# Attention values projected by token for all heads at once, in place of one head pair at a time with transposes

## The chip, the cores and the metric

The kernel runs on one core of a Trainium2 chip. The metric is the device time of one execution in microseconds (us); a median of several runs is given where there is one. Instructions are named by the engine that runs them: PE (TensorE, the matmuls), DVE (VectorE), ACT (ScalarE), POOL (GpSimd) and SP (SyncE, which here issues all the transfers).

## The reference, cut to what matters

One decoder block over 512 tokens of width 1024. The part that the change touches is the start: a norm, one wide projection, and attention over 8 heads of width 64.

```python
h = rms_norm(x, attn_norm_g[i])
u = h @ w_in[i]
u_sb, u_rw, u_gate = jnp.split(u, [SB_COLS, SB_COLS + RW_COLS], axis=-1)
q, k, v = jnp.split(u_sb.reshape(bsz, seq, 3 * SB_HEADS, SB_HEAD_DIM), 3, axis=2)
o_sb = stick_breaking_attention(q, k, v).reshape(bsz, seq, SB_WIDTH)
o_rw = rwkv7_time_mix(u_rw, ...)
```

In the attention, the weights of a block of queries are multiplied with the values: `einsum('bhqk,bhkd->bhqd', w, v)`. Behind it come a recurrent branch (`rwkv7_time_mix`), gates, an MLP and gated embeddings, and a last norm. All inputs and the output are float32.

## The kernel before

**Number format.** Every large product is made of three matmuls, because an operand is held as a high part (`hi`, fp32r) and a rest (`lo`): `hi*hi`, `hi*lo` and `lo*hi`. One such triple over 128 rows of the contraction and 512 columns is called a *step* below. `mm3` (L186 to L194) makes a step with the weights as the stationary operand, so its output has features on the partitions and tokens along the row; `rows3` (L201 to L209) makes two steps with 128 tokens of `h` as the stationary operand and the weights streaming, so its output has tokens on the partitions. A unit of weights is 128 x 1024 numbers: it comes by one transfer (`load_to`, L162), is split by one ACT copy (L175) and one DVE subtraction (L176), and serves 8 steps.

**The norm.** `h_hi` and `h_lo` hold x times the gain, without the norm's factor. The factor `rs`, one number per token, is worked out while the first products run (`rstd_of`, L260) and multiplied in when a product leaves PSUM. It lies as a [128, 512] tile with the same row of 512 tokens on each partition.

**Attention, stage 1.** The heads go in four pairs `hp`. A pair needs three units: queries, keys, values. `projected` (L390 to L416) takes a finished product out of PSUM: for queries and keys it multiplies by `rs` and splits into `hi` and `lo`; for values it only makes `vT` (L414), features by tokens. Three steps later `token_major` (L417 to L426) turns `vT` with four PE transposes (L421) and splits the result into `vv` (ACT L424, DVE L425), tokens by features. `scores` (L445) and `attend` (L484) then run for each of the 8 heads; `attend` multiplies the weights with `vv` (L497) and adds the two halves of its output into `oo` (ACT L518, DVE L519), and behind every second head a transfer writes `oo` to memory (L521).

**What sets the order.** Before the loop over the heads, the queries and keys of pair 0 (16 steps) and the values of pair 0 (8 steps) are written out. All further projections (`early`, L548) come from one generator: pairs 1 to 3 (72 steps) and then the first five units of the recurrent branch (40 steps, `early_mixes`), 112 steps in all. `drive` (L284) shares the text out between the attention of a head and 11 steps of this generator (`NSTEP = 11`), nine times: once beside the first scores, and once per head. The 13 steps that are left follow behind the last head (L573). The order on each engine is near this order of the text, but not the same: an instruction whose operands come late is set behind others that are ready. Weights are fetched two units ahead, in the order of the list `seq`.

**PSUM and SBUF.** PSUM has 8 banks: two for projections (`ps_m`), five for scores (`ps_z`), one for the output of the attention (`ps_o`). The buffers of stage 1 (`p1`) are given back as a whole when the stage ends; the buffers of stage 2 (`p2`) lie where they were.

**Stage 2, the recurrent branch.** It begins with two small products per pair (L619, L620), for which `lora_w` and `t12` are split (ACT L608, L611; DVE L609, L613). For each pair, `prepare` and `scan` make a long chain of small instructions; beside them `fill` runs the remaining projections, listed in `FILL`, five or more units for each of the five rounds, and last the product of the attention's output (`U_UPSB`). The chain ends with `o_rw` (L993), whose split (`orw`, L221 and L222) feeds the first product of stage 3.

Of the kernel before, what the change touches and what calls it, by code (L numbers as in the profile page):

```python
# [18 lines left out]
P = 128  # L19
# [66 lines left out]
def tile_block(ctx: ExitStack, tc: tile.TileContext, xT, xt, pT, wts, lora, cols_d, gfin_d, consts_d, out, dbg=None):  # L86
# [41 lines left out]
    for hp in range(HP):  # L128
        seq += [(U_QKV, hp), (U_QKV, 4 + hp), (U_QKV, 8 + hp)]
# [71 lines left out]
    def rows3(ps, w, rhs, tt, k, first, last, cs=slice(0, 512)):  # L201

        xh, xl = (r[:, :, tt * P:(tt + 1) * P] for r in rhs)
        for j in range(2):
            wh, wl = (p_.rearrange("p (j f) -> p j f", j=2)[:, j, cs] for p_ in w)
            pe.matmul(ps, xh[:, k + j], wh, start=first and j == 0, stop=False, skip_group_check=True)  # L206
# [70 lines left out]
    with ExitStack() as sA:  # L277
# [43 lines left out]
        with ExitStack() as s1:  # L321
# [62 lines left out]
            heads, late = {}, []  # L384
# [5 lines left out]
            def projected(hp, i, ps):  # L390

                if i == 0:
                    t = p1.tile([P, T], F32, name="qT", tag="qkv", bufs=3)
# [10 lines left out]
                elif i == 1:  # L404
                    t = p1.tile([P, T], F32, name="kT", tag="qkv", bufs=3)
# [6 lines left out]
                else:  # L412
                    t = p1.tile([P, T], F32, name="vT", tag="qkv", bufs=3)
                    dve.tensor_tensor(out=t, in0=ps, in1=rs, op=ALU.mult)  # L414
                    late.append([3, hp, t])

            def token_major(hp, t):  # L417

                ps = psm.tile([P, T], F32, name="ps_m")
                for j in range(4):  # L420
                    pe.transpose(out=ps[:, j * P:(j + 1) * P], in_=t[:, j * P:(j + 1) * P], identity=ident)  # L421
                vv = p1.tile([P, 4, 2, 2, 64], F32R, name="vv")
                ps4 = ps.rearrange("p (j h d) -> p j h d", j=4, h=2)
                act.copy(out=vv[:, :, :, 0, :], in_=ps4)  # L424
                dve.tensor_tensor(out=vv[:, :, :, 1, :], in0=ps4, in1=r32(vv[:, :, :, 0, :]), op=ALU.subtract)  # L425
                heads[hp] += [vv, p1.tile([P, T], F32, name="oo", bufs=1)]  # L426

            def projections(hp, which=range(3)):
                for i in which:
                    w = weights(U_QKV, i * 4 + hp)  # L430

                    ps = psm.tile([P, T], F32, name="ps_m") if (hp, i) > (1, 0) else ps_z()
# [51 lines left out]
            def attend(hp, hh, got):  # L484

                vv, oo = heads[hp][3:]
# [6 lines left out]
                def output(js):  # L493

                    for j in js:
                        for part in (wh, wl):
                            pe.matmul(ps_o[:, j * P:T], vv[:, j, hh, :, :].rearrange("p a d -> p (a d)"),  # L497
# [29 lines left out]
            pss = [psm.tile([P, T], F32, name="ps_m") for _ in range(2)]  # L527
# [3 lines left out]
            v = projections(0, (2,))  # L531
# [21 lines left out]
            def with_late(steps):  # L553

                for _ in steps:
                    for l in late[:]:
                        l[0] -= 1
                        if l[0] < 0:
                            late.remove(l)
                            token_major(*l[1:])  # L560
                    yield

            heads_ = [(hp, hh) for hp in range(HP) for hh in range(2)]
            parts = {g: {} for g in heads_}
            ahead = with_late(early())
            NSTEP = 11
            drive((3, scores(*heads_[0], parts[heads_[0]])), (NSTEP, islice(ahead, NSTEP)))
            for n, g in enumerate(heads_):
                todo = [(5, attend(*g, parts[g])), (NSTEP, islice(ahead, NSTEP))]
# [796 lines left out]
def layout(i):  # L1366
# [14 lines left out]
    def rows(w):  # L1381
# [7 lines left out]
        U_QKV: units(w_in[:, 0:1536]),  # L1389
# [36 lines left out]
```

## Time and profile before

| | us |
|---|---|
| median of 3 runs | 870.2 |
| lowest and highest | 869.28, 870.54 |
| profiled execution, its own time | 869.75 |
| its span from the first to the last instruction | 867.7 |
| PE busy in the span | 851.4 (98%) |
| DVE busy | 678.1 (78%) |
| ACT busy | 448.6 (52%) |
| POOL busy | 80.4 (9%) |

The profile is of one execution. A row of instructions gives the line of the kernel, the engine, the operation, the output, the inputs and the shape; then the count, the busy time and the mean duration. A row of the timeline gives start, duration, engine, line, operation, output and inputs, and in brackets how long the engine had been idle before and who released it. Matmuls overlap in their pipeline, so what a matmul costs is the distance from its start to the next start, not its duration.

### The profile page before, as it was taken

What the parts mean: (1) busy time and instruction counts of PE and PEld (TensorE: products, weight loads), DVE (VectorE), ACT (ScalarE), POOL (GpSimd) and SP (SyncE); (2) the same over time, 40 slices, a digit from 0 to 9 for tenths busy, and PEclk for the clock granted to TensorE, in tenths of its full rate; (3) what the DMA queues carried; (4) which work ended last, traced back from release to release, by engine and by line L of the source; (5) the groups of instructions that cost most, each with busy time, mean ns of one, the idle gap of its engine ahead of it and who ended that gap; (6) DMA issues with size and microseconds to landing.
All of it is one profiled execution on the core that took longest, in us unless ns stands there. A gap on an engine that the chain in (4) does not pass through costs nothing.

```text
span 867.7 us, 13424 instructions
## 1 busy us (share of the span) xinstructions
PE 851.4 (98%) x5182; PEld 686.8 (79%) x5182; DVE 678.1 (78%) x1228; ACT 448.6 (52%) x703; POOL 80.4 (9%) x138
## 2 busy tenths in 40 slices
PE   8999999999999999999999999999999999999996
PEld 5778787877777777777888888888888888888885
DVE  7899987896979888776754789858985987697767
ACT  6888887744335343534424464344434543453744
POOL 1432431002302111020000000000000000000000
PEclk9999999999999999999999999999999999999999
DMA  7212212221121224437935621531252034300422
GB/s 269 98 49 66 82 62 85 74 97 51 62 87 57 80 73 153 141 116 258 318 121 181 232 73 38 182 120 49 83 184 98 25 127 164 98 1 0 170 73 98
DMA packets 32272, 95.32 MB, mean 110 GB/s; under 512 B 3664, under 2 KB 3664, under 8 KB 32208
## 3 DMA queue, kind: packets, MB, share of 16 engines
q1 hardware_dynamic: 32208, 94.46, 32.6%
q8 instruction: 41, 0.67, 0.3%
q14 instruction: 23, 0.19, 0.1%
HBM read 83.96 MB, written 10.49 MB: 109 GB/s over the span
## 4 chain that ended last, share of the span: by engine, by line
PE 81%; DVE 10%; ACT 4%; issue 1%; DMA 1%; SPq 0%; POOL 0%; POOLq 0%; DVEq 0%; ACTq 0%
PE ps_m L191 13%; PE ps_m L193 13%; PE ps_m L192 13%; PE ps_m L206 9%; PE ps_m L207 9%; PE ps_m L208 9%; DVE w_lo L176 2%; PE ps_g L817 1%; PE ps_o L497 1%; PE ps_g L193 1%; PE ps_c L935 1%; PE ps_s L944 1%; PE ps_g L191 1%; PE ps_g L192 1%; PE ps_g L906 1%
## 5 line engine op out<-in xcount | busy, mean ns | idle before, releaser
L175 ACT CAST w_hi<-w_raw 128x1024 fp32r<-128x1024 f32 x94 | 99.0, 1053 | 170.4 <-PE ps_m L192 110.8
L176 DVE TENSOR_TENSOR w_lo<-w_raw,w_hi 128x1024 fp32r<-128x1024 f32 x94 | 115.1, 1225 | 37.6 <-ACT w_hi L175 37.2
L191 PE MATMUL ps_m<-h_hi,w_hi 128*128 128x512 f32 x320 | 130.6, 410 | 0.9 <-ACT h_hi L353 0.9
L192 PE MATMUL ps_m<-h_lo,w_hi 128*128 128x512 f32 x320 | 128.0, 400 | 0.0
L193 PE MATMUL ps_m<-h_hi,w_lo 128*128 128x512 f32 x320 | 127.5, 399 | 0.0
L191 PE MATMUL ps_m<-hx,w_hi 128*128 128x512 f32 x256 | 99.6, 390 | 0.4 <-ACT hx L1049 0.4
L192 PE MATMUL ps_m<-hx,w_hi 128*128 128x512 f32 x256 | 99.6, 390 | 0.0
L193 PE MATMUL ps_m<-hx,w_lo 128*128 128x512 f32 x256 | 99.5, 389 | 0.0
L191 PEld LDWEIGHTS ps_m<-h_hi,w_hi 128*128 128x128 f32 x320 | 60.7, 190 | 11.4 <-ACT h_hi L353 1.6
L193 PEld LDWEIGHTS ps_m<-h_hi,w_lo 128*128 128x128 f32 x320 | 60.3, 188 | 11.8
L192 PEld LDWEIGHTS ps_m<-h_lo,w_hi 128*128 128x128 f32 x320 | 60.5, 189 | 11.0 <-DVE h_lo L354 1.1
L191 PEld LDWEIGHTS ps_m<-hx,w_hi 128*128 128x128 f32 x256 | 48.0, 188 | 10.5 <-ACT hx L1049 0.6
L192 PEld LDWEIGHTS ps_m<-hx,w_hi 128*128 128x128 f32 x256 | 48.1, 188 | 10.2 <-DVE hx L1050 0.2
L193 PEld LDWEIGHTS ps_m<-hx,w_lo 128*128 128x128 f32 x256 | 48.0, 188 | 10.0
L207 PE MATMUL ps_m<-w_lo,fS 128*128 128x512 f32 x128 | 49.8, 389 | 0.0
L208 PE MATMUL ps_m<-w_hi,fS 128*128 128x512 f32 x128 | 49.8, 389 | 0.0
L206 PE MATMUL ps_m<-w_hi,fS 128*128 128x512 f32 x128 | 49.8, 389 | 0.0
L1291 POOL TENSOR_SCALAR r<-s 128x1 f32<-128x1 f32 x1 | 0.5, 519 | 478.9 <-DVE t L1271 478.9
L208 PE MATMUL ps_m<-w_hi,fA 128*128 128x512 f32 x96 | 37.4, 389 | 0.0
L207 PE MATMUL ps_m<-w_lo,fA 128*128 128x512 f32 x96 | 37.3, 389 | 0.0
L206 PE MATMUL ps_m<-w_hi,fA 128*128 128x512 f32 x96 | 37.3, 389 | 0.0
L221 ACT CAST fS<-sums 128x256 fp32r<-128x256 f32 (+1 forms) x32 | 19.8, 620 | 33.3 <-DVE sums L1141 33.3
(378 smaller groups left out, 1911.6 us busy)
## 6 DMA issues: line engine op xcount, KB each, us to landing
w_raw<-in_wts_dram SPq DMA_DIRECT2D x98, 512.0 KB, 3.5
gates<-gg SPq DMA_DIRECT2D x16, 256.0 KB, 2.1
x_in<-in_xT_dram SPq DMA_DIRECT2D x8, 256.0 KB, 5.7
tmp<-gates SPq DMA_DIRECT2D x8, 256.0 KB, 4.0
upsb<-tmp SPq DMA_DIRECT2D x8, 256.0 KB, 3.5
ga<-upsb SPq DMA_DIRECT2D x8, 256.0 KB, 5.4
gb<-gates SPq DMA_DIRECT2D x8, 256.0 KB, 5.4
xs<-in_xt_dram SPq DMA_DIRECT2D x4, 512.0 KB, 5.9
```

The source lines that it names most:

```text
L175: act.copy(out=hi, in_=raw)
L176: dve.tensor_tensor(out=lo, in0=raw, in1=r32(hi), op=ALU.subtract)
L191: pe.matmul(ps, wh, xh[:, k, t], start=first, stop=False)
L192: pe.matmul(ps, wh, xl[:, k, t], start=False, stop=False)
L193: pe.matmul(ps, wl, xh[:, k, t], start=False, stop=last)
L206: pe.matmul(ps, xh[:, k + j], wh, start=first and j == 0, stop=False, skip_group_check=True)
L207: pe.matmul(ps, xh[:, k + j], wl, start=False, stop=False, skip_group_check=True)
L208: pe.matmul(ps, xl[:, k + j], wh, start=False, stop=last and j == 1, skip_group_check=True)
L221: act.copy(out=hi, in_=src)
L497: pe.matmul(ps_o[:, j * P:T], vv[:, j, hh, :, :].rearrange("p a d -> p (a d)"), part[:, ZB[j]:ZB[j] + ZN[j]], start=j == 2 and part is wh, ...
L817: last = pe.matmul(ps[rows, k], left[rows, k, :], rhs[rows, k], start=True, stop=True)
L906: pe.matmul(ps[:, j * P:(j + 1) * P], Z[:, hh * 4 + g * 2 + cp, :], MA[:, g * 4 + j, :], start=True, stop=True)
```

## The change

The values of all 8 heads become one product by token: four units of weights, each with 256 rows of the contraction and all 512 columns, and four PSUM banks, one for each block of 128 tokens. They come right behind the queries and keys of pair 0. 19 of their 32 steps are written out before the first scores, 13 go into the generator in front of the queries and keys of pair 1. Each bank leaves PSUM by one ACT instruction (high part, times the factor per token) and one DVE instruction (rest). For this the factor is needed as a column, one number per partition: four DVE instructions multiply a 128 x 128 piece of `rs` with the identity and sum along the row. `vT`, the four transposes per pair and their two copies go. The shares of the generator become 16, 13 and then seven times 11; it has 101 steps when the loop begins. The queries and keys of pair 0 move to two of the five score banks. `vv` becomes one tile of 16 KB per partition in place of two of 4 KB, the buffers for `qT` and `kT` go from three to two, and a space that is kept for transfers of another kind is made smaller (`dynamic_dma_scratch_size`).

```diff
     for hp in range(HP):
-        seq += [(U_QKV, hp), (U_QKV, 4 + hp), (U_QKV, 8 + hp)]
+        seq += [(U_QKV, hp), (U_QKV, 4 + hp)]
+        if hp == 0:
+            seq += [(U_QKV, 8 + kk) for kk in range(4)]
...
-    def rows3(ps, w, rhs, tt, k, first, last, cs=slice(0, 512)):
+    def rows3(ps, w, rhs, tt, k, first, last, cs=slice(0, 512), only=None):
...
-        for j in range(2):
+        for j in range(2) if only is None else (only,):
...
-                    t = p1.tile([P, T], F32, name="vT", tag="qkv", bufs=3)
-                    dve.tensor_tensor(out=t, in0=ps, in1=rs, op=ALU.mult)
-                    late.append([3, hp, t])
-
-            def token_major(hp, t):
-
-                ps = psm.tile([P, T], F32, name="ps_m")
-                for j in range(4):
-                    pe.transpose(out=ps[:, j * P:(j + 1) * P], in_=t[:, j * P:(j + 1) * P], identity=ident)
-                vv = p1.tile([P, 4, 2, 2, 64], F32R, name="vv")
-                ps4 = ps.rearrange("p (j h d) -> p j h d", j=4, h=2)
-                act.copy(out=vv[:, :, :, 0, :], in_=ps4)
-                dve.tensor_tensor(out=vv[:, :, :, 1, :], in0=ps4, in1=r32(vv[:, :, :, 0, :]), op=ALU.subtract)
...
+            def values(pss):
+
+                for kk in range(4):
+                    w = weights(U_QKV, 8 + kk)
+                    for tt in range(4):
+                        for j in range(2):
+                            rows3(pss[tt], w, h, tt, kk * 2, kk == 0, kk == 3, only=j)
+                            yield
+                        if kk == 3:
+                            ps3 = pss[tt].rearrange("p (h d) -> p h d", h=8)
+                            r = rs_t[:, tt:tt + 1]
+                            act.activation(out=vv[:, tt, :, 0, :], in_=ps3, func=AF.Copy, scale=r)
+                            dve.scalar_tensor_tensor(out=vv[:, tt, :, 1, :], in0=ps3, scalar=r, in1=r32(vv[:, tt, :, 0, :]),
+                                                     op0=ALU.mult, op1=ALU.subtract)
...
-            pss = [psm.tile([P, T], F32, name="ps_m") for _ in range(2)]
+            pss = [ps_z() for _ in range(2)]
...
-            v = projections(0, (2,))
+
+            v = values([psm.tile([P, T], F32, name="ps_m") for _ in range(2)] + [ps_z() for _ in range(2)])
...
-            for _ in v:
+            for tt in range(4):
+                sq = p1.tile([P, T], F32, name="sq", bufs=2)[:, 0:P]
+                dve.scalar_tensor_tensor(out=sq, in0=rs[:, tt * P:(tt + 1) * P], scalar=1.0, in1=ident, op0=ALU.mult, op1=ALU.mult,
+                                         accum_out=rs_t[:, tt:tt + 1])
+            for _ in islice(v, 18):
                 pass
...
             def early():
+                yield from v
                 for hp in range(1, HP):
                     yield from projections(hp)
                 yield from early_mixes()
...
-            NSTEP = 11
-            drive((3, scores(*heads_[0], parts[heads_[0]])), (NSTEP, islice(ahead, NSTEP)))
+            NSTEP = [16,13] + [11] * 7
+            drive((3, scores(*heads_[0], parts[heads_[0]])), (NSTEP[0], islice(ahead, NSTEP[0])))
...
-    nc = bacc.Bacc("TRN2", target_bir_lowering=False, num_devices=1)
+    nc = bacc.Bacc("TRN2", target_bir_lowering=False, num_devices=1, dynamic_dma_scratch_size=2048)
```

More of the change, by code (lines that the diff above doesn't have):

```diff
@@ L382, in c1 @@
                 return first[:, COFF[k] - NCONST:COFF[k] - NCONST + P]
-            heads, late = {}, []
+            heads = {}
+            vv = p1.tile([P, 4, 8, 2, 64], F32R, name="vv", bufs=1)
+            rs_t = p1.tile([P, 4], F32, name="rs_t", bufs=1)
             qls = [[p1.tile([P, T], F32R, name=f"ql{n}{hh}", bufs=1) for hh in range(2)] for n in range(2)]
@@ L403, in projected @@
                     heads[hp] = [qq, ql]
-                elif i == 1:
-                    t = p1.tile([P, T], F32, name="kT", tag="qkv", bufs=3)
+                else:
+                    t = p1.tile([P, T], F32, name="kT", tag="qkv", bufs=2)
                     dve.tensor_tensor(out=t, in0=ps, in1=rs, op=ALU.mult)
@@ L411, in projected, with projections @@
                     heads[hp].append(kk)
[L412 to L429 removed]
+            def values(pss):
[11 more added lines that the diff above has]
+                                                     op0=ALU.mult, op1=ALU.subtract)
+            def projections(hp):
+                for i in range(2):
                     w = weights(U_QKV, i * 4 + hp)
[L432 removed]
+                    ps = psm.tile([P, T], F32, name="ps_m")
                     yield from product_steps(ps, w, h)
@@ L484, in attend @@
             def attend(hp, hh, got):
-                vv, oo = heads[hp][3:]
+                if hh == 0:
+                    heads[hp].append(p1.tile([P, T], F32, name="oo", bufs=1))
+                oo = heads[hp][3]
                 sl = HALVES[hh]
@@ L496, in output @@
                         for part in (wh, wl):
-                            pe.matmul(ps_o[:, j * P:T], vv[:, j, hh, :, :].rearrange("p a d -> p (a d)"),
+                            pe.matmul(ps_o[:, j * P:T], vv[:, j, hp * 2 + hh, :, :].rearrange("p a d -> p (a d)"),
                                       part[:, ZB[j]:ZB[j] + ZN[j]], start=j == 2 and part is wh, stop=j == 0 and part is wl,
@@ L551, in early @@
                 yield from early_mixes()
[L553 to L561, printed above, removed]
             heads_ = [(hp, hh) for hp in range(HP) for hh in range(2)]
             parts = {g: {} for g in heads_}
-            ahead = with_late(early())
-            NSTEP = 11
-            drive((3, scores(*heads_[0], parts[heads_[0]])), (NSTEP, islice(ahead, NSTEP)))
+            ahead = early()
+            NSTEP = [16,13] + [11] * 7
+            drive((3, scores(*heads_[0], parts[heads_[0]])), (NSTEP[0], islice(ahead, NSTEP[0])))
             for n, g in enumerate(heads_):
-                todo = [(5, attend(*g, parts[g])), (NSTEP, islice(ahead, NSTEP))]
+                todo = [(5, attend(*g, parts[g])), (NSTEP[n + 1], islice(ahead, NSTEP[n + 1]))]
                 if n + 1 < len(heads_):
@@ L1388, in layout @@
         U_PLE: rows(a["w_ple_proj"][0]),
-        U_QKV: units(w_in[:, 0:1536]),
+        U_QKV: np.concatenate([units(w_in[:, 0:1024]), rows(w_in[:, 1024:1536])], 0),
         U_RW: units(w_in[:, 1536:3328]),
```

2 lines of the change are left out of this document (1 added, 1 removed).

## The prediction, made before the result was known

> **What bounds the kernel now.** I read the page first, then busy time by stretches, then the timeline of PE around the lines that change, the chain of waits, and the end of stage 2.
>
> ```profile
> span 867.7 us, 13424 instructions
> PE 851.4 (98%) x5182; PEld 686.8 (79%) x5182; DVE 678.1 (78%) x1228; ACT 448.6 (52%) x703; POOL 80.4 (9%) x138
> ...
> 30.00:50.00 20.00, 19.11 (x95) 14.15 (x95) 19.41 (x37) 18.61 (x37) 8.44 (x12) 1.00 0.23 77
> 50.00:140.00 90.00, 89.11 (x457) 72.90 (x457) 80.65 (x148) 74.02 (x136) 27.17 (x43) 1.00 0.18 62
> ...
> 150.00:200.00 50.00, 49.42 (x361) 38.72 (x363) 42.69 (x82) 27.00 (x40) 1.04 (x3) 1.00 0.26 85
> ```
>
> The columns of the last three rows are stretch, length, then busy us of PE, weight loads, DVE, ACT and POOL, then the granted clock (1.00), the transfers' share and GB/s. PE is the bound in every stretch; in the first 20 us of the attention DVE (19.41 of 20) and ACT (18.61) are nearly as full. So a matmul taken out is worth its distance to the next start, if PE still has work in order, and a late DVE can take the gain back.
>
> The execution shown took 869.75 us, 2.05 us more than its span; the median of the runs is 870.2, 0.45 above it. I sum differences and put them on the median. A difference under 0.2% (1.74 us) counts as no change.
>
> **1. The transposes go.**
>
> ```profile
> L421 PE MATMUL ps_m<-cst,vT x16: 271/272/328, 30.4 to 115.0; 128*128 128x128 f32 x16
> ...
> 57.57 0.39 PE L193 MATMUL ps_m<-h_hi,w_lo 128*128 128x512 f32 x1
> 57.80 0.60 PE L421 MATMUL ps_m<-cst,vT 128*128 128x128 f32 x4
> 58.15 0.48 PE L191 MATMUL ps_m<-h_hi,w_hi 128*128 128x512 f32 x1
> 58.47 0.40 PE L192 MATMUL ps_m<-h_lo,w_hi 128*128 128x512 f32 x1
> ...
> 30.43 0.66 PE L421 MATMUL ps_m<-cst,vT 128*128 128x128 f32 x4 [0.35 <-DVE vT L414]
> ```
>
> The first row is all sixteen (shortest, median and longest in ns, first and last start), the others are the timeline. From 57.57 to 58.47 are 0.90 us, in which there are also two plain matmuls of 0.23 each (57.57 to 57.80), so a group of four costs 0.44 us. Four groups: -1.78 us. The group at 30.43 had also made PE idle for 0.35: -0.35. The next late thing there is the keys of pair 0, which the change leaves, and PE has values to project until they come.
>
> The Trainium skill, page "TensorE: Matmul & The Clock Gate", section "Part 4: PE-mode transpose", gives about 275 ns for a transpose inside a kernel. The median duration of 272 agrees with it, but four start within 0.35 us, so the duration is not the cost here; at 275 each sixteen would give an estimate of 4.4.
>
> **2. The product itself costs the same.** 4 pairs x 8 steps were 32, and now 4 units x 4 banks x 2 are 32, three matmuls of 512 columns each. With `h` stationary instead of the weights there is a row from stage 3:
>
> ```profile
> L206 PE MATMUL ps_m<-w_hi,mg x64: 388/389/390, 426.0 to 468.8; 128*128 128x512 f32 x64
> ```
>
> The same 0.39 as in the rows above: 0. The transfers are the same units in the same queue, in another order, two units ahead as before: 0. The smaller space concerns transfers of a queue of which the profile shows none, as all data go by one kind:
>
> ```profile
> q1 hardware_dynamic: 32208, 94.46, 32.6%
> ```
>
> **3. DVE and ACT in stage 1.**
>
> ```profile
> L414 DVE TENSOR_TENSOR vT<-ps_m,rs x3: 683/684/685, 53.3 to 111.4; 128x512 f32<-128x512 f32 x3
> ...
> L424 ACT CAST vv<-ps_m x4: 567/587/587, 31.8 to 115.7; 128x512 fp32r<-128x512 f32 x4
> L425 DVE TENSOR_TENSOR vv<-ps_m,vv x4: 683/690/692, 33.3 to 116.3; 128x512 fp32r<-128x512 f32 x4
> ...
> L305 ACT ACTIVATE mix<-u,omm x12: 719/724/729, 138.4 to 272.1; 128x512 f32<-128x512 f32 x12
> ...
> L354 DVE SCALAR_TENSOR_TENSOR h_lo<-x_in,cols,h_hi x8: 742/743/752, 5.9 to 15.9; 128x512 fp32r<-128x512 f32 x8
> ...
> L478 DVE TENSOR_TENSOR sums<-sp x8: 278/284/286, 37.8 to 126.2; 128x128 f32<-128x128 f32 x8
> ```
>
> Gone from DVE: 4 x (0.68 + 0.69) = 5.5 us; from ACT 4 x 0.59 = 2.4. Added: four splits with a factor per partition, by the nearest rows 4 x 0.72 = 2.9 on ACT and 4 x 0.74 = 3.0 on DVE; and four sums for the column, which no row shows, between 0.28 (128 columns, no sum) and 0.74: 1.1 to 3.0. I take 1.4, as they are 128 wide. DVE gets 5.5 - 3.0 - 1.4 = 1.1 us lighter in sum, heavier at the start, and lighter by 1.37 per pair later.
>
> At the start, the four sums stand behind the splits of pair 0 and ahead of the scores' work; PE has 13 more steps (3 x 0.23 x 13 = 9 us) of values that need nothing but weights. The third block of scores and the next head's first take banks that the last two blocks of tokens held: such a bank is free 0.72 + 0.74 = 1.5 us behind its last matmul, and PE has in that time the last block's six matmuls (1.4) and the queries of pair 1. I take +0.2 in all, between 0 and +1.5. Queries and keys of pair 1 move behind the values, to the end of the second share; the scores that need them stand right behind. The keys' way out (L406, two copies on ACT, two subtractions on DVE) is some 2.7 us by rows like the above, and the 11 steps of the share behind (7.5 us) hide it; without that cover it would cost 2.7 once.
>
> Later, PE waited twice for DVE in pair 2:
>
> ```profile
> 94.70 0.38 PE L497 MATMUL ps_o<-wh,vv 128*128 128x256 f32 x1 [0.29 <-DVE wh L511]
> 95.63 0.39 PE L497 MATMUL ps_o<-wl,vv 128*128 128x256 f32 x1 [0.55 <-DVE wl L512]
> ```
>
> In each pair DVE loses L414 and L425 (1.37 us) ahead of such work. I take half of the 0.84: -0.4, between -0.84 and 0.
>
> **4. The hand-over to stage 2.** This is what could turn the sign. The generator has 101 steps for shares of 16 + 13 + 7 x 11 = 106, so nothing is left behind the last head; before, 13 steps were.
>
> ```profile
> 139.09 0.40 PE L497 MATMUL ps_o<-wl,vv 128*128 128x512 f32 x1
> 139.32 0.39 PE L191 MATMUL ps_m<-h_hi,w_hi 128*128 128x512 f32 x1
> ...
> 148.85 0.39 PE L619 MATMUL ps_g<-lx,lw 128*128 128x512 f32 x1
> ```
>
> The chain of waits has in the same stretch (start, length, what):
>
> ```profile
> 140.47 0.70 DVE oo L519
> ...
> 141.18 2.99 DMA o_sb<-oo
> ...
> 149.08 0.68 DVE lxl L613
> ...
> 149.90 0.47 PE ps_g L620
> ```
>
> Between 139.32 and 148.85 lie 42 matmuls (9.53 / 42 = 0.227 each), 14 steps. Under them runs a chain: the last output, `oo`, its transfer, and only then the buffers of stage 2, up to the second L620 at 149.90, 10.8 us behind the last output. As the text leaves 13 steps there and PE had 14, PE kept to the text's order through the attention. Now the same steps lie ahead of the last output: it moves from 139.1 to about 148.6 less the 2.1 saved, 146.5, or to 144.5 if the last head, with 6 steps in place of 11, draws ahead. The chain then reaches its second L620 not at 149.9 but at 155.3 to 157.3, less a microsecond or so where ACT and DVE are free of the old tail: 5 to 7 us later.
>
> PE is not idle in that gap if it takes the first round of `fill`, 40 steps (27 us) that need only stage 1's leftovers. It has run ahead so before:
>
> ```profile
> 203.16 0.69 DVE L304 TENSOR_TENSOR u<-ps_m,rs 128x512 f32<-128x512 f32 x1 [0.15 <-PE ps_m L193]
> ```
>
> That takes out the seventh unit of `fill`, while the first round, whose chain was still running, has five. So the recurrent chain starts 5 to 7 us late, with PE as much ahead in filling; the debt falls due at the end of stage 2:
>
> ```profile
> 396.28 0.63 PE L987 MATMUL ps_c<-cst,y 128*128 128x128 f32 x4
> 404.19 0.39 PE L191 MATMUL ps_m<-orw,w_hi 128*128 128x512 f32 x1
> 406.23 0.39 PE L191 MATMUL ps_m<-orw,w_hi 128*128 128x512 f32 x1
> ...
> 398.73 0.63 ACT L667 ACTIVATE tmp<-tmp 128x512 f32<-128x512 f32 x1 [2.69 <-DMA tmp<-gates]
> 399.27 0.76 ACT L989 ACTIVATE yf<-ps_c,cols 128x512 f32<-128x512 f32 x1
> ...
> 402.06 1.22 DVE L176 TENSOR_TENSOR w_lo<-w_raw,w_hi 128x1024 fp32r<-128x1024 f32 x1
> 403.20 0.68 DVE L222 TENSOR_TENSOR orw<-o_rw,orw 128x512 fp32r<-128x512 f32 x1
> ```
>
> The chain ends with the last split, 403.20 + 0.68 = 403.9; its product needs pair 3's part first at 406.23. That is 2.3 us of slack. The chain can also be pulled in: L989 could have run at about 397 instead of 399.27, but stood behind L667, which waited for a transfer (2.2), and the last split stood behind a weight split (1.2). And the second product of L191 can give PE nine matmuls (2.0) that need only pairs 0 to 2. Together 7.7, less the 2.1 by which PE comes there earlier: 5.6 against a delay of 5 to 7. I take +0.3; the ends are 0 and, with slack alone and the full delay, 7 - 2.3 = +4.7 over the time before, which eats the saving too.
>
> **Sum:** -1.78 - 0.35 - 0.4 + 0.2 + 0.3 = -2.03. 870.2 - 2.0 = 868.2 us.
>
> **The rivals.**
>
> *The debt shows in part.* If only the slack and one of the two ways to pull in work (2.3 + 2.0 or 2.3 + 3.4, less 2.1), 2.2 to 3.6 us of a delay of 6 are covered, and 2.4 to 3.8 show. Against a saving of 2.3 ahead of that term this gives 870.2 + 0.1 to + 1.5: 870.3 to 871.7, no change. For it: the chain has DVE at 42.69 of 50 all along, which leaves little room to catch up. Against: the waits at 398.73 and 402.06 come from filling, which will be done earlier.
>
> *The hand-over decides: slower.* Place: the last output, its transfer, the buffers of stage 2. With a delay of 7, no catching up and no second product early, 4.7 us more: 874.9; with a delay of 5, 872.9. It decides from a delay, net of what is caught up, of 2.3: from there the time is above the time before. For it: the chain of waits runs through `oo`, its transfer and L613. The Trainium skill, page "Perfetto Trace Analysis", section "Optimization Strategy", says that a gap that repeats on the engine that should be full can mean that there is no room for the next tile; here DVE's gap of 3 us under the transfer comes once, and PE has none, so no run here shows that case.
>
> *More than the transposes.* If both waits at 94.70 and 95.63 go, and nothing is lost at either end: -1.78 - 0.35 - 0.84 = -3.0, 867.2. If transposes held PE for their whole duration, 16 x 0.272 = 4.4 and the rest would give -5.1, 865.1; the start at 58.15, 0.35 behind the first, speaks against it.
>
> *It does not do what it says.* The transposes surely go, but DVE at the start (19.41 of 20) may pass on more than 0.2: with the four sums at 0.74 each and a bank waited for, 1.5 + 1.6 = 3.1 instead of 0.2, less 0.35 and 1.78 and 0.4: 870.2 + 0.9 = 871.1, no change.
>
> **How the numbers follow.** Forecast with its neighbour of larger gain: 0.40 and 0.07. The debt in part 0.24, the crowded start 0.07: no change. The hand-over in full 0.19; 0.03 for the rest of slower cases. Forecast cases near -1.7 fall on either side, so I move 0.02 to no change: faster 0.45, same 0.33, slower 0.22. The range takes in the larger gain without the long transposes, down to 866.8, and the hand-over somewhat past its lower end, 873.4. The forecast's own range is 867.2 to 869.
>
> **What would show it.** Right: no L421; PE from about 30 to 140 without a wait of over 0.3; the last L497 at 144 to 147; under the transfer of `oo` PE full with L191 to L193 into `ps_m`, and L620 near 155; at the end of stage 2 no wait of PE for `orw`, and stage 3 starting near 402. Wrong: idle PE behind the last L497, a wait of PE for `orw` of over 1 us (then the hand-over decided), or waits of L458 and L497 between 32 and 60 (then the start did). If the last L497 stays near 139, step 4 fails as a whole.

## The result and the profile after

The changed kernel takes 877.4 us (median of 6 runs, 875.52 to 879.02) against 870.2 (6 runs, 869.28 to 870.54): 1.0085 times the time before, with a 95% interval of 1.0075 to 1.0096. The forecast was 868.2 and its range ended at 873.4: the change was to gain 2.0 us, and it costs 7.2. The profiled execution took 877.11 us, its span is 875.0. One execution in each of two experiments below ran at a granted clock of 0.56 and took 1399 and 1403 us; these times are left out, and of the second of these kernels there is no other profile.

The head of the page of the changed kernel:

```profile
span 875.0 us, 13401 instructions
PE 851.9 (97%) x5166; PEld 685.1 (78%) x5166; DVE 679.0 (78%) x1232; ACT 450.9 (52%) x703; POOL 81.0 (9%) x138
```

Its busy time by the same three stretches as before (length, then PE, weight loads, DVE, ACT, POOL, granted clock, share and GB/s of the transfers):

```profile
30.00:50.00 20.00, 20.00 (x97) 16.34 (x96) 15.43 (x29) 13.82 (x26) 2.99 (x6) 1.00 0.30 93
50.00:140.00 90.00, 87.43 (x440) 70.12 (x439) 80.04 (x149) 74.32 (x138) 30.41 (x47) 1.00 0.19 65
150.00:200.00 50.00, 48.19 (x231) 37.38 (x230) 41.83 (x71) 31.37 (x48) 4.84 (x15) 1.00 0.25 85
```

The sixteen transposes are gone (5182 less 5166 matmuls). In the first stretch PE is now full (20.00, before 19.11), and DVE, which was nearly full, rests for 4.6 us (15.43 busy, before 19.41). In the second PE has lost 1.7 us of busy time (87.43, before 89.11), in the third 1.2.

The hand-over, in the timeline of PE and DVE. Line numbers have moved: L497 is now L502, L619 and L620 are L620 and L621, L519 is L524, L191 is L193.

```profile
148.64 0.50 PE L502 MATMUL ps_o<-wl,vv 128*128 128x512 f32 x1
148.97 0.39 PE L193 MATMUL ps_m<-h_hi,w_hi 128*128 128x512 f32 x1
...
155.57 0.47 PE L620 MATMUL ps_g<-lx,lw 128*128 128x512 f32 x1
...
150.13 0.68 DVE L524 TENSOR_TENSOR oo<-ps_o,oo 64x512 f32<-64x512 f32 x1 [0.38 <-ACT oo L523]
153.29 0.20 DVE L837 COPY X<-cst 128x64 f32<-128x64 f32 x1 [0.34 <-DMA o_sb<-oo]
```

The last output stands at 148.64 (before 139.09). The first write into the buffers of stage 2 (153.29) waits for the transfer of `oo`. As foretold, PE does not rest under this transfer: it goes on with L193 to L195. From there to the end of stage 2 three points of the recurrent chain can be set side by side: its first exponential (ACT), the key's norm of pairs 0 and 3 (DVE L713, now L714), and the last split. Of the kernel before:

```profile
156.59 0.63 ACT L695 ACTIVATE gx<-w 128x512 f32<-128x512 f32 x1
...
167.73 0.75 DVE L713 SCALAR_TENSOR_TENSOR tmp<-mix,cols,tmp 128x512 f32<-128x512 f32 x1
...
318.77 0.75 DVE L713 SCALAR_TENSOR_TENSOR tmp<-mix,cols,tmp 128x512 f32<-128x512 f32 x1
```

and of the changed one, with the first product of stage 3 below (before at 404.19):

```profile
163.66 0.64 ACT L696 ACTIVATE gx<-w 128x512 f32<-128x512 f32 x1
...
174.86 0.75 DVE L714 SCALAR_TENSOR_TENSOR tmp<-mix,cols,tmp 128x512 f32<-128x512 f32 x1
...
327.96 0.75 DVE L714 SCALAR_TENSOR_TENSOR tmp<-mix,cols,tmp 128x512 f32<-128x512 f32 x1
...
410.64 0.69 DVE L224 TENSOR_TENSOR orw<-o_rw,orw 128x512 fp32r<-128x512 f32 x1 [0.93 <-ACT orw L223]
...
411.37 0.39 PE L193 MATMUL ps_m<-orw,w_hi 128*128 128x512 f32 x1
```

The chain starts 7.1 us late (163.66 against 156.59) and is 7.1, 9.2 and 7.4 late at the other points; stage 3 starts 7.2 late. That is the whole loss: 877.4 - 870.2 = 7.2. Over these 250 us, taken together, nothing was caught up.

### The profile page after: what moved, and what is told of

It reads as the page before. It is cut to its first block, busy times and chain, and to the rows that moved or that the text cites. A ratio compares the mean times of both kernels' runs of the same rounds, so it can differ in the third digit from the quotient of the medians.

```text
span 875.0 us, 13401 instructions
## 1 busy us (share of the span) xinstructions
PE 851.9 (97%) x5166; PEld 685.1 (78%) x5166; DVE 679.0 (78%) x1232; ACT 450.9 (52%) x703; POOL 81.0 (9%) x138
## 4 chain that ended last, share of the span: by engine, by line
PE 77%; DVE 14%; ACT 5%; issue 2%; DMA 1%; SPq 0%; POOL 0%; POOLq 0%; DVEq 0%; ACTq 0%
PE ps_m L193 12%; PE ps_m L195 11%; PE ps_m L194 11%; PE ps_m L208 10%; PE ps_m L209 10%; PE ps_m L210 10%; DVE w_lo L178 2%; PE ps_g L907 1%; DVE LX L839 1%; PE ps_g L818 1%; PE ps_c L936 1%; DVE own L829 1%; DVE sp L469 1%; DVE S L953 1%; DMA w_raw<-in_wts_dram 1%
## 5 line engine op out<-in xcount | busy, mean ns | idle before, releaser
L193 PE MATMUL ps_m<-h_hi,w_hi 128*128 128x512 f32 x288 | 117.3, 407 | 0.1
L195 PE MATMUL ps_m<-h_hi,w_lo 128*128 128x512 f32 x288 | 115.5, 401 | 0.0
L194 PE MATMUL ps_m<-h_lo,w_hi 128*128 128x512 f32 x288 | 114.9, 399 | 0.0
L193 PE MATMUL ps_m<-hx,w_hi 128*128 128x512 f32 x256 | 99.6, 390 | 0.4 <-ACT hx L1050 0.4
L195 PE MATMUL ps_m<-hx,w_lo 128*128 128x512 f32 x256 | 99.5, 389 | 0.0
L195 PEld LDWEIGHTS ps_m<-h_hi,w_lo 128*128 128x128 f32 x288 | 54.2, 188 | 10.8
L193 PEld LDWEIGHTS ps_m<-h_hi,w_hi 128*128 128x128 f32 x288 | 54.6, 189 | 9.0 <-DVE gg L679 0.3
L194 PEld LDWEIGHTS ps_m<-h_lo,w_hi 128*128 128x128 f32 x288 | 54.3, 189 | 9.0
L193 PEld LDWEIGHTS ps_m<-hx,w_hi 128*128 128x128 f32 x256 | 48.0, 188 | 10.6 <-ACT hx L1050 0.6
L195 PEld LDWEIGHTS ps_m<-hx,w_lo 128*128 128x128 f32 x256 | 48.0, 188 | 9.9
```

The lines of the kernel that those rows point to most:

```text
L193: pe.matmul(ps, wh, xh[:, k, t], start=first, stop=False)
L194: pe.matmul(ps, wh, xl[:, k, t], start=False, stop=False)
L195: pe.matmul(ps, wl, xh[:, k, t], start=False, stop=last)
```

## The experiments

Each time is a median; the kernel before was run beside it on the same chip (870.1, 869.8, 869.5 and 869.7 in the four sets), and each ratio is to that.

**The hand-over.** *13 steps left behind the last head again* (changed kernel):

```diff
-            NSTEP = [16,13] + [11] * 7
+            NSTEP = [16, 13, 9, 9, 8, 8, 8, 8, 9]
```

> The changed kernel with shares of 16, 13, 9, 9, 8, 8, 8, 8 and 9 steps, so that 13 of the 101 steps are left behind the last head, as before. Theory A (the chain of stage 2 starts late because nothing is left behind the last head): the first L620 goes from 155.6 back to about 148, and the time to 868 to 870. Theory B (the queries and keys of pairs 1 to 3, now packed closer together, make PE wait for DVE in the attention): the start of stage 2 moves, but some 3 us of waits stay, 871 to 874. Theory C (the values' four banks at the start): no change, 877.

Measured 874.5 (1.0053, 1.0040 to 1.0066). The chain starts at 157.7, 1.1 late, but its end, `o_rw`, is 4.3 late (405.2 against 400.9). So theory A was right about the start of stage 2 (its first small product, L620, is back at 150.0), but not about the time: only 2.9 us came back, and something else took time later in this run (it is named below, at the place in the instruction stream).

*No step left behind in the kernel before:*

```diff
-            NSTEP = 11
+            NSTEP = [18, 17] + [11] * 7
```

> The kernel before, values and transposes as they were, with shares of 18, 17 and seven times 11, so that all 112 steps lie ahead of the end of the last head and none behind it. Theory A: it loses what the change lost and the saved transposes besides, the last L497 at about 147 to 148 and 876 to 879. Theories B and C: no loss, 870 to 871.

Measured 873.6 (1.0046, 1.0033 to 1.0060), a loss as in theory A, but smaller: the last output comes at 145.0 and not at 147 to 148. The chain starts at 159.83, 3.2 late, and stage 3 starts 3.3 late. So the late start alone, without any change of the values, costs what it is late.

*`oo` kept in `o_rw`, so that stage 2 need not wait for its transfer,* in the changed kernel and in the kernel before (there the same edit in `token_major`):

```diff
-                    heads[hp].append(p1.tile([P, T], F32, name="oo", bufs=1))
+                    heads[hp].append(o_rw[:, hp, :])
```

> The changed kernel with the output of each pair of heads written into the buffer of the recurrent branch's output, which is free until late in stage 2, so that stage 2's buffers need not wait for the transfer of that output (150.84 to 153.2). Theory A: the start of stage 2 comes 2.4 us earlier and so does the end, about 875.0. Theories B and C: no change, 877.4.

> The same move of the output's buffer in the kernel before. If the chain of stage 2 sets the end of the stage there too, the start comes up to 3 us earlier (L620 was held by L614's forerunner until 149.8) and the time falls to 867.5 to 868.5. If PE's work sets it, as the prediction had it, no change: 869.7 to 870.7.

Measured 874.6 (1.0052, 1.0040 to 1.0065) and 869.3 (0.9988, 0.9979 to 0.9997). In the changed kernel the chain starts 2.0 earlier, near the 2.4 of theory A. In the kernel before, where the 13 steps cover the transfer, it starts 0.7 earlier, but this is not shown to be the edit: PE is 0.68 ahead already at the first scores (31.97 against 32.65), and `oo` is first written behind them. Of the versions that leave nothing out of the computation it is the one that is faster than the kernel before, by 0.1%, below what I count as a change.

**The attention.** *The kernel before without its transposes:* L421 and its bank are left out and `vv` is split from `vT`, so the values stand in the wrong layout.

```diff
-                ps = psm.tile([P, T], F32, name="ps_m")
-                for j in range(4):
-                    pe.transpose(out=ps[:, j * P:(j + 1) * P], in_=t[:, j * P:(j + 1) * P], identity=ident)
...
-                ps4 = ps.rearrange("p (j h d) -> p j h d", j=4, h=2)
+                ps4 = t.rearrange("p (j h d) -> p j h d", j=4, h=2)
```

> The kernel before without its four transposes per pair: `vv` is split straight from `vT`, so the values stand in the wrong layout (the transposes are left out of the computation). It measures the saving alone. Theory of the prediction (PE sets the pace of the attention, each group of four costs 0.44 and the first 0.35 more): 870.2 - 2.1 = 868.1. Rival (the heads' work on DVE and ACT sets the pace, so PE only waits longer): 869.5 to 870.5, with the last output within 0.5 of 139.5.

Measured 872.5 (1.0026, 1.0013 to 1.0039): slower, which neither theory allowed. On PE and DVE the order of stage 2 is the same as before, so the instructions can be laid side by side: they run 0.74 us ahead from 140 on (PE had 0.54 of this at 22, where nothing had been left out yet), and then, at one group of 64 small matmuls near 300, fall behind. That group, in the kernel before and in this one (timeline of PE):

```profile
298.91 1.10 PE L817 MATMUL ps_g<-LX,LB 32*32 32x64 f32 x64
299.94 0.50 PE L192 MATMUL ps_m<-h_lo,w_hi 128*128 128x512 f32 x1
```

```profile
298.30 0.84 PE L814 MATMUL ps_g<-LX,LB 32*32 32x64 f32 x47
300.70 0.35 PE L814 MATMUL ps_g<-LX,LB 32*32 32x64 f32 x9 [1.56 <-issue]
300.99 0.50 PE L192 MATMUL ps_m<-h_lo,w_hi 128*128 128x512 f32 x1
```

Nine matmuls before the end of the group PE stops for 1.56 us; "issue" means that it waited for nothing that the profile shows. Just behind it the clock falls, as busy time in stretches of 1 us shows (the third column from the right is the granted clock):

```profile
301.00:302.00 1.00, 1.00 (x8) 0.81 (x5) 0.91 (x3) 0.47 (x1) 0.00 (x0) 0.78 0.05 16
302.00:303.00 1.00, 1.00 (x7) 0.35 (x6) 1.00 (x2) 1.00 (x2) 0.00 (x0) 0.50 0.00 0
...
304.00:305.00 1.00, 1.00 (x7) 0.81 (x3) 0.89 (x2) 0.00 (x0) 0.00 (x0) 0.51 0.59 225
305.00:306.00 1.00, 1.00 (x35) 0.65 (x33) 0.97 (x4) 0.00 (x0) 0.00 (x0) 1.00 0.00 0
```

The stop leaves PE 1.05 us behind the kernel before at the end of the group (300.99 against 299.94), and the 3.4 us at half clock take it to 2.1. The kernel with 13 steps left had the same: 1.49 near 302, another 0.93 near 359, and a halved clock from 359 to 363.

*The scores of head 0 behind 7 steps of the values in place of 19* (with 13 steps left; the values take the bank of `ps_o` for one block, and the shares become 10, 16, 15 and then 8 or 9):

```diff
-            for _ in islice(v, 18):
+            for _ in islice(v, 6):
...
+            second = scores(*heads_[1], parts[heads_[1]])
+            drive((1, islice(second, 1)), (16, islice(ahead, 16)))
```

> Changed kernel with 13 steps left behind the last head, and the scores of head 0 put behind 7 of the 32 steps of the values in place of 19 (the values take the bank of the output for one block of tokens, so that the scores have banks). Theory C (the values stand ahead of the scores, so DVE and ACT idle for some 5 us between 30 and 50, and are then late for the heads that follow): DVE is busy for 18 or more of the 20 us from 30 to 50 (14.9 with the scores behind), the outputs of pairs 1 to 3 come 1 to 3 us earlier, the time falls from 874.5 to 871.5 to 873.5. Theory D (the queries and keys of a pair, packed into 16 steps ahead of their scores, make the waits): no waits go, 874 to 875.

Measured 877.6 (1.0092, 1.0076 to 1.0108). The first scores come at 30.4 (35.4 in the changed kernel), but the first output still at 51.9 (51.7), since it needs all 32 steps of the values; DVE is busy for 15.7 of the 20 us. Theory C fell as put: DVE did not reach the 18 us that it asked for, and the last output came 3.0 us later (143.2 against 140.2 with 13 steps left alone). Its time cannot be set against the 874.5 of that kernel as it stands, since the stops differ: this profile has one of 1.72 us near 306, with 6.8 us at half clock behind it.

*DVE made lighter by 14 us* in the kernel before and in the changed kernel with 13 steps left: the rest of the attention's weights is left out of the computation.

```diff
-                    dve.tensor_tensor(out=wl[:, s:s + n], in0=sp[:, s:s + n], in1=r32(wh[:, s:s + n]), op=ALU.subtract)
...
-                        for part in (wh, wl):
+                        for n_, part in enumerate((wh, wh)):
```

> The kernel before with the rest of the attention's weights left out of the computation: no subtraction on DVE for `wl`, and the product that took `wl` takes `wh` a second time, so PE has the same matmuls and DVE some 14 us less. Theory PE (in the kernel before PE sets the pace of the attention): only the two waits of 0.84 in sum and a shorter end go, the last output comes at 137.5 to 139 in place of 139.1, the time is 868.5 to 869.5. Theory DVE (DVE sets it there too): the last output comes 3 us or more earlier, at 136 or before, though PE has 98% busy in these stretches.

> The changed kernel with 13 steps left behind the last head, and the same rest of the weights left out of the computation (same matmuls, 14 us less on DVE). Theory DVE (with the transposes gone and the values first, DVE with the heads' chain sets the pace from 60 to 140, and this hid what PE saves): PE's waits there go, the last output moves from 140.2 to 135 to 137, and the chain of stage 2 starts 3 us or more earlier than in the kernel with `wl`. Rival (the waits come from banks, weights or the packed queries and keys): the last output stays within 1 us of 140.

Measured 868.4 (0.9991, 0.9982 to 1.0000; only the time is used here) and 871.8 (1.0031, 1.0019 to 1.0043). The first time lies just below the range of theory PE (868.5 to 869.5); the place of the last output, which was to tell the two theories apart, was not seen. So in the kernel before 14 us less on DVE are worth some 1.1. In the second the last two outputs begin at 138.3 in place of 140.0, a greater move than the rival allowed (1 us) and a smaller one than the 3 to 5 us of theory DVE, and the chain starts 1.7 earlier; its time holds a stop of 1.80 near 301. Busy time from 60 to 140 of the kernel before, of the changed kernel, of it with 13 steps left, and of that without the rest:

```profile
60.00:140.00 80.00, 79.11 (x403) 64.45 (x402) 71.75 (x131) 66.21 (x121) 24.79 (x38) 1.00 0.19 63
```

```profile
60.00:140.00 80.00, 77.43 (x389) 61.96 (x389) 71.23 (x134) 67.11 (x125) 26.08 (x43) 1.00 0.19 63
```

```profile
60.00:140.00 80.00, 75.99 (x384) 60.48 (x383) 73.50 (x139) 68.80 (x130) 26.67 (x42) 1.00 0.17 57
```

```profile
60.00:140.00 80.00, 76.97 (x392) 62.02 (x391) 63.99 (x119) 69.88 (x132) 23.85 (x40) 1.00 0.17 57
```

PE loses 3.1 us of busy time with the values first and 13 steps left (79.11 to 75.99). Taking 9.5 us off DVE in this stretch brings back 1.0 of them. So DVE's load is a part of the cause, and the rest was not found.

**The place in the instruction stream.** The kernels that had the gap have 16 matmuls fewer ahead of stage 2. *Two of the twelve warm-up matmuls at the very start are replaced by 18 narrow ones,* so that the count is as before:

```diff
-            for _ in range(12):
+            for _ in range(10):
                 pe.matmul(ps, warm[:, 0:P], warm, start=True, stop=True)
+            for _ in range(18):
+                pe.matmul(ps[:, 0:16], warm[:, 0:P], warm[:, 0:16], start=True, stop=True)
```

It was tried on the kernel without transposes, and on the changed kernel with both edits of the hand-over, which had run without it first.

> Changed kernel with 13 steps left behind the last head and `oo` held in `o_rw` (both edits of the two runs before). Theory A (the time is lost where the attention hands over, and each edit mends its own part of that): the two gains add, 877.4 - 2.9 - 2.9 = 871.7, stage 2's chain begins at 155 to 156. Theory A' (both edits mend the same microseconds): 873.5 to 874.5. Theory B (what is left is lost in the attention, where DVE is late): the last output still lies at 140, and 871.5 or more stays.

> The kernel before without its transposes (left out of the computation, as in the earlier run of that kind), and with two of the twelve warm-up matmuls replaced by 18 narrow ones, so that PE has as many instructions ahead of stage 2 as the kernel before. Theory place (the gap of 1.56 us without a visible cause inside a group of 64 small matmuls near 300, and the halved clock that follows it, depend on how many PE instructions stand ahead): both go, the 0.74 us gained by 140 last to the end, 868.9 to 869.4. Rival (the gap comes from time or chance): it stays near 300, 870.3 to 872.5.

> The changed kernel with 13 steps left, `oo` in `o_rw`, and the same 18 narrow warm-up matmuls in place of two wide ones, so as many PE instructions ahead of stage 2 as before. Theory place: the gap of 1.58 near 302 goes, the delay of 1.0 at the start of stage 2's chain is the delay at its end, 870.5 to 871.5 (873.5 to 875.7 without the padding). Rival: the gap stays, 873 to 875.5.

With both edits of the hand-over, without the padding 875.0 (1.0056, 1.0044 to 1.0068; the last output stays at 140.1, as theory B had it), with it 871.5 (1.0024, 1.0015 to 1.0033). The kernel without transposes goes from 872.5 to 869.5 (0.9997, 0.9987 to 1.0007). The same group without the gap, in the padded kernel without transposes:

```profile
298.31 1.10 PE L816 MATMUL ps_g<-LX,LB 32*32 32x64 f32 x64
```

It starts at 298.31 as before the padding (298.30) and ends in one piece. Theory place holds: 3 to 3.5 us, more than the change was to bring, hang on how many instructions stand ahead. (Of the 3.5 only 1.8 lie between the first and the last instruction, by the medians of the spans, 871.4 and 869.6. The rest lies outside the span and was not explained.)

The traces also show what goes on at such a stop. The profile lists a transfer queue of the kind "instruction", here on the page of the kernel before:

```profile
q8 instruction: 41, 0.67, 0.3%
```

These are 41 transfers of 16,384 bytes, one to 255 of the 10,459 records of PE (matmuls, weight loads and its sequencer's own). In all experiments together PE stopped fifteen times between 25 and 860 us for over 0.4 us with "issue" as the reason, for 0.46 to 2.06 us. Counted from the start, each stop stands in front of PE's record 2242, 3266, 4290 or 5570 or the one behind it, and these lie 4, 4 and 5 times 256 apart. In front of each, a transfer of this queue had ended 1.2 to 1.6 us before PE went on. So PE had most likely run through a block of 256 instructions before the next had come. Not every border between blocks shows it, as the kernel before has no such stop; the padding moves the borders by 32 records, out of a burst of small matmuls or into one.

The worth of the sixteen transposes in the kernel before can now be read, too: none in the time. The padded kernel without them runs 0.6 us ahead at the start of stage 2, but DVE had this lead at 27 already, before the first transpose (30.43), because a unit of weights, for which ACT waited in the kernel before, had come earlier. The copy of that unit in the kernel before, and in this one:

```profile
26.27 1.05 ACT L175 CAST w_hi<-w_raw 128x1024 fp32r<-128x1024 f32 x1 [1.63 <-DMA w_raw<-in_wts_dram]
```

```profile
25.61 1.05 ACT L175 CAST w_hi<-w_raw 128x1024 fp32r<-128x1024 f32 x1 [0.96 <-PE ps_z L192]
```

**The changed kernel and its repairs once more, padded.** Without the padding, the repairs of the hand-over and that gap could not be told apart.

> The changed kernel with two of the twelve warm-up matmuls replaced by 18 narrow ones, as many PE instructions ahead of stage 2 as in the kernel before; nothing else. Its profile without this shows only one gap without a visible cause, of 0.29 us. Theory hand-over (the 7.3 us come from the late start of the recurrent chain): 876.5 to 877.8. Rival (the place in the instruction stream, as in the kernels with 13 steps left): 873.5 to 875.

> The changed kernel with 13 steps left behind the last head, and the padding. Theory hand-over: the chain of stage 2 starts 1.1 us later than before and ends 1.1 us later, 870.8 to 871.9, so that leaving no step behind the last head costs 5.5 to 6.5 us. Rival (leaving the steps is worth only the 2.9 us that it gave without the padding): 873.5 to 874.5.

> The changed kernel with `oo` in `o_rw`, none left behind the last head, and the padding. Its profile without the padding showed no gap to be mended, so 874.0 to 875.2, 2 to 3 us under the padded changed kernel: what the transfer under the hand-over costs. Rival (the padding is worth 3 us everywhere): 871 to 872.

| changed kernel, padded | us | ratio to before, 95% | chain starts | stage 3 starts |
|---|---|---|---|---|
| as it is | 877.2 | 1.0088 (1.0075 to 1.0102) | 163.3 | 411.6 |
| `oo` in `o_rw` | 876.1 | 1.0075 (1.0062 to 1.0088) | 161.5 | 409.7 |
| 13 steps left | 871.1 | 1.0018 (1.0008 to 1.0027) | 158.0 | 405.5 |

The padding changes nothing in the time of the changed kernel itself. There the gap is 0.29 near 260 without padding and 1.55 near 258 with it, and the time is the same; the second row has one of 1.63, the third has none. Leaving 13 steps behind is worth 877.2 - 871.1 = 6.1 us, of which the missing gap may be one or so. Keeping `oo` in `o_rw` alone is worth 1.0, not the 2 to 3 expected (1.9 by the profiled executions, 2.9 without the padding). On top of the 13 steps it is worth nothing (871.5, in the run further up): both edits mend the same microseconds. With 13 steps left the instructions of stage 2 are in the order of before and run about 1.3 us late from 150 to the last stage. The chain's points in that run:

```profile
158.03 0.63 ACT L698 ACTIVATE gx<-w 128x512 f32<-128x512 f32 x1
...
169.14 0.75 DVE L716 SCALAR_TENSOR_TENSOR tmp<-mix,cols,tmp 128x512 f32<-128x512 f32 x1
...
320.12 0.75 DVE L716 SCALAR_TENSOR_TENSOR tmp<-mix,cols,tmp 128x512 f32<-128x512 f32 x1
```

Late by 1.4, 1.4 and 1.35: what stage 2 gets late it hands on late, to the tenth.

**Could the debt be caught up?** In the changed kernel PE stops three times in the first rounds of stage 2, each time when 5, 10 and 15 units of `fill` are done, which is when the next would need a buffer that the chain still holds:

```profile
182.10 0.51 PE L642 MATMUL ps_g<-tmp,bones 128*128 128x512 f32 x1 [1.43 <-ACT tmp L638]
...
228.53 0.49 PE L936 MATMUL ps_c<-S,Q 128*128 128x128 f32 x2 [1.00 <-DVE S L953]
...
281.46 0.49 PE L936 MATMUL ps_c<-S,Q 128*128 128x128 f32 x2 [1.03 <-DVE S L953]
```

*A third buffer for what the filling leaves* (`u`, `gg`, and the two tiles of stage 3 that share them), without and with the padding:

```diff
-                gg = pa.tile([P, T], F32, name="gg", bufs=2)
+                gg = pa.tile([P, T], F32, name="gg", bufs=3)
```

> Changed kernel with three buffers in place of two for what the filling products leave (`gg`, `u`). Theory cap (PE ran ahead by the debt, but stops at 5, 10 and 15 units because their buffers are full, so the debt is paid there): the stops of 1.4, 1.0 and 1.0 us near 182, 228 and 281 go, and the time falls by 1 to 3 us, to 874.5 to 876.5. Theory chain (the recurrent chain alone sets the end, however much PE has filled): the stops move or go, but the last split and the first product of stage 3 stay within 0.5 of 411.4, and the time stays within 1 of 877.4.

> The changed kernel with three buffers for what the filling products leave, and the padding. Without it this kernel had a gap of 1.31 near 261 and then a halved clock near 376. Theory cap (the debt of the late start can be caught up if PE may fill further ahead): 872 to 874, so 3 us or more under the padded changed kernel. Rival (the chain alone sets the end, more filling ahead only gets in its way): 875 or more.

Measured 875.8 (1.0062, 1.0050 to 1.0074) and 878.2 (1.0090, 1.0078 to 1.0103). Without the padding this is 1.6 less than with two buffers, within the range of theory cap; with it, 1.0 more (878.2 against 877.2). In both the three stops go, and PE has filled 10.2 units in place of 9.3 at the key's norm of pair 1. But the chain comes there later still: by 2.5 us without the padding (225.9 against 223.4, with no "issue" gap of over 0.4 until there), by 4.1 with it (227.1 against 223.0, a gap of 1.64 included). Stage 3 starts at 410.3 and 411.1, in place of 411.4 and 411.6. Of the padded profiles the one with two buffers has one gap of the "issue" kind (1.55), the one with three has two (1.64 and 2.06) and 3.4 us at half clock, so this pair does not settle how much a third buffer can bring back. That the chain comes later because more filling stands in its way is argued.

## Why the prediction was wrong

*Step 1, the transposes (-1.78 and -0.35).* PE was taken as the bound in every stretch, and the work was taken at its distance on PE. That price holds: laid beside the kernel before, the padded kernel without the transposes gains 0.43 to 0.45 us on PE at each of the last three groups. But PE gives it back at the next waits for the weights of a head (`wh`, `wl`): it is 1.05 ahead at 92 and 0.27 at 95. These waits from 30 to 150 (sum, times, longest), in the kernel before and in the padded one without transposes:

```profile
PE ps_o L497 <- DVE wl L512: 0.7, 2, 0.5
PE ps_o L497 <- DVE wh L511: 0.3, 1, 0.3
```

```profile
PE ps_o L496 <- DVE wh L510: 1.9, 3, 1.1
PE ps_o L496 <- DVE wl L511: 0.5, 1, 0.5
```

So PE and the path through DVE bind by turns, and less work on one of them alone brings little: 14 us less on DVE brought some 1.1, sixteen transposes less on PE brought nothing in the time.

*Step 2, the product itself (0).* It holds: the 16 matmuls of a kind into score banks have a median of 389 ns, as in stage 3, and in the timeline they start 0.23 us apart, which is the price.

```profile
L208 PE MATMUL ps_z<-w_hi,h_hi x16: 389/389/473, 23.1 to 42.7; 128*128 128x512 f32 x16
```

*Step 3, DVE and ACT (+0.2, -0.4, and the keys' way out at 0).* The prices hold: the splits are 0.68 and 0.74 us, the four sums 0.29 and 0.08 for reading the sum out, 1.5 in all where 1.4 was taken. Their effect did not. At the start nothing was crowded; the 0.9 us that PE had rested from 30 to 50 went, more than forecast, and the first output came at 51.74 in place of 41.66, because PE now does all heads' values first. DVE rested meanwhile, and its work for the heads was pushed behind. The waits from 60 to 140, by engine and line waited for (sum, times, longest), in the kernel before, the changed one, and the changed one with 13 steps left and padded:

```profile
PE ps_o L497 <- DVE wl L512: 0.5, 1, 0.5
PE ps_o L497 <- DVE wh L511: 0.3, 1, 0.3
```

```profile
PE ps_o L502 <- DVE wl L517: 1.1, 2, 0.6
PE ps_z L461 <- DVE kk L414: 1.0, 1, 1.0
PE ps_o L502 <- DVE wh L516: 0.3, 1, 0.3
```

```profile
PE ps_z L463 <- DVE kk L416: 1.3, 2, 1.0
PE ps_o L504 <- DVE wh L518: 0.8, 1, 0.8
PE ps_z L516 <- DVE spl L224: 0.8, 2, 0.4
PE ps_z L512 <- DVE spl L224: 0.4, 1, 0.4
PE ps_o L504 <- DVE wl L519: 0.3, 1, 0.3
```

From 0.8 they grow to 2.4 and 3.6, where the forecast had half of the 0.8 going away. The keys (`kk`), moved behind the values, were not covered by the 11 steps as said: PE stops a whole microsecond for them at the scores (L461). So, with 13 steps left, the attention gives back what PE saved by the transposes and 1.4 us more (871.1 against 869.7). That DVE's load is a part of it is shown; what makes the rest is open. That the values, done first, are then missing as filling between the later heads is only argued, and the smaller pool for `qT` and `kT` (two buffers in place of three) and the moved banks were not tried alone.

*Step 4, the hand-over (+0.3).* This is the step that failed. Its first half held: the steps of the generator moved ahead of the last output, PE filled on under the transfer, and the delay, forecast as 5 to 7, was 7.1 (the last output came at 148.6, forecast as 144 to 147, since the 2.1 saved ahead of it were lost). Its second half said that the chain starts late "with PE as much ahead in filling" and that the debt falls due at the end, where "Together 7.7, less the 2.1 by which PE comes there earlier: 5.6 against a delay of 5 to 7" would cover it. What was covered measured 0. The lead was there at first and did not last. At the same point of the chain, PE had done more matmuls of filling than in the kernel before by 33 at the first exponential and at the key's norm of pair 0 (7.5 us at 0.227 each), by 34 at pair 1, 25 at pair 2, 12 at pair 3 (2.7 us), and by 4 (0.9 us) at the chain's last small products, which came 8.1 late (404.34 against 396.28):

```profile
404.34 0.63 PE L988 MATMUL ps_c<-cst,y 128*128 128x128 f32 x4 [0.66 <-DVE y L983]
```

Behind these, PE had 25 matmuls of filling left, against 29 before, and only then came to the product of stage 3, 7.2 late. So the slack of 2.3 at the last split was worth nothing: the product did not wait for `orw` in either kernel, it waited for its turn on PE. With 13 steps left (padded) these counts are those of the kernel before, to one matmul. The debt did not fall due at the end; it was paid along the way, as idle PE. Busy time from 150 to 410, the sums of four stretches, before and after:

```profile
sum 260.00, PE 256.03 PEld 199.55 DVE 209.38 ACT 117.71 POOL 36.91; mean PE 64.01 PEld 49.89 DVE 52.34 ACT 29.43 POOL 9.23
```

```profile
sum 260.00, PE 250.74 PEld 192.63 DVE 210.31 ACT 120.34 POOL 41.12; mean PE 62.68 PEld 48.16 DVE 52.58 ACT 30.09 POOL 10.28
```

PE is busy for 5.3 us less there. Of the signs of a wrong forecast that the prediction named, PE idle right behind the last output and a wait for `orw` were not there; the sign was the 48.19 of 50 in the stretch behind. Of the signs of a right one, stage 3 did not start near 402, and PE had a wait of 0.98 in the attention. That the chain could not catch up because DVE is busy for 209 of the 260 us, beside a PE that had 256, fits the rows but was not tested. The rival "the hand-over decides" had the right mechanism and still gave the chain 2.3 us of slack (at most 874.9); with 7.1 late, none of it back, and no saving ahead of it, its own working gives 870.2 + 7.1 = 877.3.

The loss, divided by the padded runs (877.15, 871.10 and 869.74): 6.05 us for the hand-over and 1.36 for the attention. This is near and not exact, as the edit that leaves 13 steps also changes the shares within the attention.

## What to carry to other kernels

Independent matmuls that stand behind the last result of one stage are the cover for the start of the next; to write them ahead of it delays that start, and here all of the delay came out at the end of the next stage. A lead of PE in filling can be lost on the way: count it at several points of the chain, not at its start alone. An operation taken off the fullest engine is worth its time only if the next engine in the same chain has room: look at the second fullest in each stretch before the saving is booked. And before a difference of 0.3% is given a cause, look in each profile for PE stops of the "issue" kind, and for what an engine was ahead by before the edit could act. Padding to the old instruction count took such stops from three kernels here and gave one to the changed kernel.

## What the runs showed of the hardware

PE could stop for 0.5 to 2.1 us without a cause in the program, mostly inside a group of small matmuls: fifteen times in these runs, each time at a border that lies a multiple of 256 PE instructions from the others, and 1.2 to 1.6 us after a transfer of 16,384 bytes in the queue of the kind "instruction" had ended. That PE waits there for its next block of instructions is inferred from these times. Padding of 32 records (16 matmuls and 16 weight loads), put at the very start, took the stop away from three kernels; on two of them it was tried for that, and took 3.0 and 3.5 us off their medians.

A stop could be followed by a granted clock of one half, for 3.4 us (6.8 in one profile). In the unpadded kernel without transposes the three runs at a mean clock of 0.998 took 870.3 to 871.2 us, the four at 0.995 872.4 to 872.6, and the one at 0.991 876.1; one at 0.997 took 873.5. The Trainium skill, page "TensorE: Matmul & The Clock Gate", section "Part 1: The HAM clock gate", puts the fall to half rate behind an idle window of about 3.4 us. No rest of PE ahead of the five falls seen here was that long (0.93 to 1.72 us), and seven other rests of 1.55 to 1.80 us had no fall behind them, so what sets it off stays open.
